# Two heads' attention output as one half-by-half matmul group, with the softmax weights scaled on GpSimd

## The chip, the cores and the metric

The kernel runs on one core of a Trainium2 chip. The metric is the device time of one execution in microseconds (us), as the median of several runs. TensorE (PE in the rows) does matrix products, VectorE (DVE) and ScalarE (ACT) elementwise work and the copies out of PSUM, the accumulator memory; GpSimd (POOL) does a little elementwise work in SBUF, the working memory,. SyncE (SP) issues the weight transfers.

## What is computed

Two layers of a decoder trunk over 512 tokens of width 1024. In each layer one projection feeds four token mixers, whose outputs are gated and summed. The change concerns one of them, sparse attention with 4 heads of 64 dimensions over query blocks of 128 tokens. Cut to what matters:

```python
logits = jnp.einsum('bqhd,bqkhd->bhqk', qb, ks) * (ATT_HD ** -0.5)   # the 128 selected keys of each query
logits = jnp.where(valid[:, None], logits, -jnp.inf)
p = jax.nn.softmax(logits, axis=-1)
y_b = jnp.einsum('bhqk,bqkhd->bqhd', p, vs)                           # -> (512 tokens, 4 heads * 64)
...
merged = merged + gates[:, :, 1] * (y_b @ w_branch[1])
```

The kernel does not gather: it adds a large number to the logits of keys that are not selected, so that block b of queries works on all W = (b+1)*128 keys up to its own.

## The kernel before

All large products go through `mm3`: three passes of a split operand pair (`whi`/`wlo` weights, `hh`/`hl` activations) with 512 columns streaming, in groups called `g` (gate projections), `p` (branch projections), `up`, `dn`, `wo`, `fm`, `tk`. Each engine runs its instructions in the order in which the program stands; the wait for an operand holds up all that is queued behind it on that engine.

The mixers run as generators in the list `side`. `fm_group` calls `tick()` after 4 and after 8 of its 8 weight slices, and each tick advances every generator to its next `yield`. So between two ticks TensorE has either 12 matmuls of `g`, or 6 of `p` and then 12 of `g`. Attention is started ahead of `gates(3, ...)` and one step of it is done at each tick. Its result `yb` is first read by `gates(1, ...)`, a whole gate branch later.

Before, `attention` goes through 16 pairs (block b, head h), four heads in each block. A step i issues, in this order: for every fourth pair `out`, then `values` of pair i-2, `transp` of pair i-1, `softmax` of pair i.

- `softmax`: two matmuls give the logits `lg` in PSUM; DVE adds the selection and takes a row minimum (`L`, `mn`); ACT takes the exponential of `L` and its row sum (`se`); DVE inverts `se`. `L` stays unscaled.
- `transp`: TensorE transposes `L` in blocks of 128 (tile `pT` in PSUM), one ACT copy brings the whole of it to SBUF.
- `values`: for each key block a matmul with the transposed weights in the array and 64 columns of values (`vt`) streaming; result `av` (queries on partitions, 64 columns). DVE scales it by `se` on the way out (`yt`).
- `out`: two transposes (`yT`) turn a block's 256 columns of `yt` back to features on partitions; ACT and DVE split them into `yh` and `yl`.

`mix`, `U` and `br` are small products of other mixers. `mix` and `U` put 64 columns of weights in one half of the array's columns and the next product's in the other half, by the partitions they write (`half(j)`).

Of the kernel before, what the change touches and what calls it, by code (L numbers as in the profile page):

```python
# [13 lines left out]
F32 = mybir.dt.float32  # L14
F32R = mybir.dt.float32r
BF16 = mybir.dt.bfloat16
AF = mybir.ActivationFunctionType
ALU = mybir.AluOpType
# [3 lines left out]
P = 128  # L22
D = 1024
T = 512
# [341 lines left out]
def mixer(tc, em, env):  # L366
# [9 lines left out]
    def et(name):  # L376
        return yp.tile([P, T], F32, name=name, tag="e", bufs=8)

    def ytile(n):
        return (yp.tile([P, 2, T], F32R, name=f"yh{n}", tag="yh", bufs=3),  # L380
                yp.tile([P, 2, T], F32R, name=f"yl{n}", tag="yl", bufs=3))

    tscope = ExitStack()
    tp = tscope.enter_context(tc.tile_pool(name="tp", bufs=1))
    ts = tscope.enter_context(tc.tile_pool(name="ts", bufs=1))

    def tt(shape, name, bufs=1, tag=None):

        p_ = ts if int(np.prod(shape[1:])) % T else tp
        return p_.tile(shape, F32, name=name, tag=tag or name, bufs=bufs)  # L390
# [2 lines left out]
        rs, rb = env["rs"], env["rb"]  # L393

    def rtile(name):
        return tp.tile([P, T], F32R, name=name, tag="ix", bufs=8)

    def half(h):
        return slice((h % 2) * 64, (h % 2) * 64 + 64)

    def blk(c):
        return slice(c * P, (c + 1) * P)
# [18 lines left out]
    def fm_proj():  # L421
        w_h, w_l = next_w()
        pt = mmtile("fm")
        fm_group(pt, w_h, w_l, hh, hl)
        return pt
# [41 lines left out]
    if l > 0:  # L467
        pq = tok_proj(512, G1K, [1, 2, 3], MM4)
    else:

        x0, acc = [], []
        raw01 = yp.tile([P, 2, T], F32R, name="raw01", tag="yh", bufs=3).bitcast(F32)

        def first_loads(k0):
            ks = {0: (0, 1), 1: ()}.get(k0, (k0, k0 + 1))
            for k in ks:
                x0.append(rtile("x0").bitcast(F32))
                with HP():
                    nc.sync.dma_start(x0[k], x_in[k])
                acc[:] = [norm(x0, lp("ln_mix"), hh, hl, (k,), *acc, sq_hp=False, sq_tile=et)]  # L480
            return raw01[:, k0] if k0 < 2 else None

        pq = tok_proj(512, G1K, [1, 2, 3], MM4, first_loads)
        load_consts()
        rs, rb = rstd(acc[0])
# [16 lines left out]
    def table(n):  # L502
# [8 lines left out]
                           ALU.mult, ALU.mult)  # L511
    qiT = {}
    kiT = rtile("kiH"), rtile("kiL")

    def indexer_prep():
# [19 lines left out]
        for c in (1, 2, 3):  # L535
            pk = mmtile("qiT", "ms")
            for j in range(4):
                ptr(pk[:, blk(j)], qr[c][:, blk(j)])

            a, b = qiT[c] = rtile("qiA"), rtile("qiB")  # L540
            lo = et("qiL").bitcast(F32R)
            stack(a, b, pk, (lo[lower], lo[upper]))
            stack_move(a, b, lo[lower], lo[upper])
            yield
# [8 lines left out]
    def indexer(b, sco):  # L553

        W = (b + 1) * P
        for h in range(8):
            pt = mmtile("ix", "ms")
            for i in range(2):
                pmm(pt[:, :W], qiT[b][h % 2][:, blk(h // 2)], kiT[i][:, :W], i == 0, i == 1)
            rel = tt([P, T], "rel", 3, "X")  # L560
            S.activation(rel[:, :W], pt[:, :W], AF.Relu)
            w = wx[:, b, h:h + 1]
            if h == 0:
                V.tensor_scalar(sco[:, :b * P], rel[:, :b * P], w, 0.0, ALU.mult, ALU.add)
                V.scalar_tensor_tensor(sco[:, b * P:], rel[:, b * P:W], w, negP, ALU.mult, ALU.add)
            else:
                V.scalar_tensor_tensor(sco, rel[:, :W], w, sco, ALU.mult, ALU.add)
            if h % 2 == 1:
# [9 lines left out]
        V.tensor_scalar(sco, sco, SENT, BIG, ALU.not_equal, ALU.mult)  # L578

    def attention(sel, yb):  # L580
        yt, Ls, pTs = {}, {}, {}

        def softmax(b, h):
            W = (b + 1) * P
            pt = mmtile("lg", "ms")
            j = h // 2
            q, k = qS[h % 2][:, j, blk(b)], kS[h % 2]
            pmm(pt[:, :W], q, k[:, j, :W], True, False)
            pmm(pt[:, :W], q, kL[h % 2][j][:, :W], False, True)
            L = rtile("L").bitcast(F32)  # L590
            mn = tt([P, 1], "mn", 2)
            se = tt([P, 1], "se", 4)
            V.tensor_tensor_reduce(L[:, :W], pt[:, :W], sel[b], 1.0, 3.4e38, ALU.add, ALU.min, mn)
            S.activation(L[:, :W], L[:, :W], AF.Exp, bias=mn, scale=-1.0, accum_out=se)
            V.reciprocal(se, se)
            Ls[b, h] = (L, se)

        def transp(b, h):
            W = (b + 1) * P
            pk = mmtile("pT", "ms")  # L600
            for s in range(b + 1):
                ptr(pk[:, blk(s)], Ls[b, h][0][:, blk(s)])
            pT = rtile("pT").bitcast(F32)
            S.copy(pT[:, :W], pk[:, :W])
            pTs[b, h] = pT

        def values(b, h):
            if h == 0:
                yt[b] = tt([P, 4, 64], "yt", 2)
            po = mmtile("av", "ms")  # L610
            for s in range(b + 1):
                pmm(po[:, 0:64], pTs[b, h][:, blk(s)], vt[:, s, h * 64:(h + 1) * 64], s == 0, s == b)
            V.tensor_scalar(yt[b][:, h], po[:, 0:64], Ls[b, h][1], None, ALU.mult)

        def out(b):
            pk = mmtile("yT", "ms")
            y2 = yt[b].rearrange("p h d -> p (h d)")
            for j in range(2):
                ptr(pk[:, blk(j)], y2[:, blk(j)])
            pv = pk[:, 0:256].rearrange("p (j t) -> p j t", j=2)  # L620
            yh, yl = yb[0][:, :, blk(b)], yb[1][:, :, blk(b)]
            S.copy(yh, pv)
            V.tensor_sub(yl, pv, yh.bitcast(F32))

        seq = [(b, h) for b in range(4) for h in range(4)]
        for i in range(len(seq) + 3):
            if i >= 3 and seq[i - 3][1] == 3:
                out(seq[i - 3][0])
            if 2 <= i < len(seq) + 2:
                values(*seq[i - 2])  # L630
            if 1 <= i < len(seq) + 1:
                transp(*seq[i - 1])
            if i < len(seq):
                softmax(*seq[i])
            yield
# [160 lines left out]
    def tops():  # L796
        for b, per in ((1, 2), (2, 1), (3, 1)):
# [5 lines left out]
    qS, kS = ([tp.tile([P, 2, T], F32R, name=f"{n}S{r}") for r in range(2)] for n in "qk")  # L803
    hp = env["hpool"]
    kL = ([tp.tile([P, T], F32R, name=f"kL0{j}") for j in range(2)],
          [hp.tile([P, T], F32R, name=f"kL1{j}", tag=("acc", "sq")[j]) for j in range(2)])
# [59 lines left out]
    vt = tt([P, 4, 256], "vt")  # L866
# [10 lines left out]
    for i in range(2):  # L877
        pt = fm_proj()
        with HP():
            V.tensor_mul(cqT[:, i], pt, rb)  # L880
    for i in range(2):
        pt = fm_proj()
# [31 lines left out]
    for c2 in range(2):  # L914
        t = et("gv")
# [34 lines left out]
    for i in range(2):  # L950
        pt = fm_proj()
        u2, t = et("u2"), et("gu")
# [8 lines left out]
    for i in range(2):  # L961
        dc, z, db, t = et("dc"), et("z"), et("db"), et("cv")
        for j, dst in enumerate((dc, z, db)):
            pt = fm_proj()
# [38 lines left out]
    gates(0, ya, 0)  # L1003
    yb = ytile(1)
    side.append(attention(sel, yb))
    gates(3, yd, 1)
    gates(2, yc, 2)
# [9 lines left out]
    for m in range(KD):  # L1017
        w_h, w_l = next_w()
        pt = mmtile("wo")
# [96 lines left out]
```

## Time and profile before

| | |
|---|---|
| median of 3 runs | 1659.71 us (1659.55 to 1659.79) |
| the profiled execution | 1658.94 us |
| its span, first to last instruction | 1657.2 us |
| TensorE busy | 1650.9 us |
| VectorE busy | 956.3 us |
| ScalarE busy | 585.0 us |
| GpSimd busy | 66.0 us |
| mean granted TensorE clock | 0.999 |

The span is what the instructions take; the 1.7 us around it are launch and end. An engine's busy time is the union of its instructions. Of TensorE's instructions the ends are modelled and neighbours overlap, so the steps from one start to the next tell what one costs, not the durations.

### The profile page before, as it was taken

How to read it: one execution, taken by the hardware profiler on the slowest of the kernel's cores; microseconds unless marked ns; L12 is line 12 of the kernel's file. 1: busy time of each engine (PE TensorE's matmuls, PEld its weight loads, DVE VectorE, ACT ScalarE, POOL GpSimd, SP SyncE). 2: the span in 40 equal slices, each digit the busy share in tenths (PEclk: the TensorE clock that was granted, in tenths of full speed). 3: DMA queues.
4: the chain of work that ended last, by engine and by line, in shares of the span. 5: the costliest groups of instructions: out<-in, count | busy, mean ns of one | idle time of the engine just before them, and what ended most of it. 6: DMA issues, size and time to landing. Idle time of an engine off the chain costs nothing.

```text
span 1657.2 us, 20279 instructions
## 1 busy us (share of the span) xinstructions
PE 1650.9 (100%) x7958; PEld 1373.5 (83%) x7958; DVE 956.3 (58%) x1727; ACT 585.0 (35%) x876; POOL 66.0 (4%) x81
## 2 busy tenths in 40 slices
PE   9999999999999999999999999999999999999999
PEld 7888788888888888888888877888888888888888
DVE  6899886555554423443358999855555544334422
ACT  5543233423334312342235432244233343123311
POOL 1311000000000000000012110000000000000000
PEclk9999999999999999999999999999999999999999
DMA  5432222243232323323334222221422323233231
GB/s 205 121 90 90 80 80 80 80 133 98 84 108 89 102 90 101 101 90 121 114 117 121 78 93 92 77 83 64 147 92 89 96 95 102 91 100 101 91 127 64
DMA packets 49296, 164.74 MB, mean 99 GB/s; under 512 B 5680, under 2 KB 8496, under 8 KB 49200
## 3 DMA queue, kind: packets, MB, share of 16 engines
q1 hardware_dynamic: 45072, 158.76, 29.6%
q0 software_dynamic: 3264, 3.67, 1.1%
q8 instruction: 63, 1.03, 0.3%
q10 hardware_dynamic: 864, 1.01, 0.2%
q14 instruction: 33, 0.27, 0.1%
HBM read 155.55 MB, written 4.19 MB: 96 GB/s over the span
## 4 chain that ended last, share of the span: by engine, by line
PE 100%; POOL 0%; ACT 0%; DVE 0%; ACTq 0%; issue 0%
PE g L132 21%; PE dn L132 21%; PE up L132 21%; PE tk L132 10%; PE fm L132 8%; PE p L132 5%; PE wo L132 5%; PE ix L132 1%; PE av L132 1%; PE lg L132 1%; PE pT L132 1%; PE Gb L132 1%; PE intra L132 0%; PE inter L132 0%; PE S L132 0%; PE cols L132 0%
## 5 line engine op out<-in xcount | busy, mean ns | idle before, releaser
L132 ACT CAST whi<-raw 128x1024 fp32r<-128x1024 f32 (+3 forms) x270 | 293.3, 1086 | 636.0 <-PE dn L132 252.0
L132 DVE TENSOR_TENSOR wlo<-raw,whi 128x1024 fp32r<-128x1024 f32 (+3 forms) x270 | 342.2, 1268 | 174.3 <-ACT whi L132 166.6
L132 PE MATMUL dn<-al,whi 128*128 128x512 f32 (+1 forms) x528 | 202.0, 383 | 0.0
L132 PE MATMUL dn<-ah,wlo 128*128 128x512 f32 (+1 forms) x528 | 202.0, 383 | 0.0
L132 PE MATMUL dn<-ah,whi 128*128 128x512 f32 (+1 forms) x528 | 202.0, 383 | 0.0
L132 PE MATMUL g<-hl,whi 128*128 128x512 f32 x512 | 200.6, 392 | 0.0
L132 PE MATMUL g<-hh,whi 128*128 128x512 f32 x512 | 200.6, 392 | 0.0
L132 PE MATMUL g<-hh,wlo 128*128 128x512 f32 x512 | 200.1, 391 | 0.0
L132 PE MATMUL up<-hh,whi 128*128 128x512 f32 x512 | 199.6, 390 | 0.0
L132 PE MATMUL up<-hh,wlo 128*128 128x512 f32 x512 | 199.2, 389 | 0.0
L132 PE MATMUL up<-hl,whi 128*128 128x512 f32 x512 | 199.2, 389 | 0.0
L132 DVE SCALAR_TENSOR_TENSOR u<-up,rb 128x512 f32<-128x512 f32 x64 | 44.1, 691 | 158.9 <-PE up L132 158.9
L132 PEld LDWEIGHTS dn<-al,whi 128*128 128x128 f32 x528 | 99.2, 188 | 19.4
L132 PEld LDWEIGHTS dn<-ah,whi 128*128 128x128 f32 x528 | 99.2, 188 | 19.4
L132 PEld LDWEIGHTS dn<-ah,wlo 128*128 128x128 f32 x528 | 99.2, 188 | 19.2
L132 PEld LDWEIGHTS g<-hh,wlo 128*128 128x128 f32 x512 | 96.3, 188 | 20.3
L132 PEld LDWEIGHTS up<-hh,wlo 128*128 128x128 f32 x512 | 96.1, 188 | 20.1
L132 PEld LDWEIGHTS up<-hl,whi 128*128 128x128 f32 x512 | 96.1, 188 | 20.0
L132 PEld LDWEIGHTS up<-hh,whi 128*128 128x128 f32 x512 | 96.1, 188 | 19.7
L132 PEld LDWEIGHTS g<-hl,whi 128*128 128x128 f32 x512 | 96.2, 188 | 19.6
L132 PEld LDWEIGHTS g<-hh,whi 128*128 128x128 f32 x512 | 96.1, 188 | 19.6
L132 PE MATMUL tk<-whi,hh 128*128 128x512 f32 (+2 forms) x304 | 107.8, 357 | 0.0
(253 smaller groups left out, 2492.2 us busy)
## 6 DMA issues: line engine op xcount, KB each, us to landing
raw<-in_wall_dram SPq DMA_DIRECT2D x194, 512.0 KB, 3.4
raw<-in_wall_dram SPq DMA_DIRECT2D x64, 640.0 KB, 3.9
x<-in_x_dram SPq DMA_DIRECT2D x16, 256.0 KB, 5.0
raw<-in_wall_dram SPq DMA_DIRECT2D x8, 336.0 KB, 2.9
x_dram<-x SPq DMA_DIRECT2D x8, 256.0 KB, 2.0
x<-x_dram SPq DMA_DIRECT2D x8, 256.0 KB, 6.7
out_dram<-x SPq DMA_DIRECT2D x7, 256.0 KB, 2.0
raw<-in_wall_dram SPq DMA_DIRECT2D x4, 256.0 KB, 3.3
```

Of the source, the lines that this page charges most:

```text
L132: r = f(*a, **k)
```

## The change

`attention` now goes by pairs of heads: j is the pair, r the head in it, and the order is j, then block b, then r. A `softmax` ends with a GpSimd instruction that multiplies `L` by the inverted row sum in SBUF; the transposes read that. The transposed weights of all four query blocks of a head are collected in three SBUF tiles (`p0` for key block 0, `p1` for key block 1, `p23` for key blocks 2 and 3), so that `transp` has up to three ACT copies instead of one. `values` is issued twice in a layer, once for each pair of heads: values (64 columns) sit in the array, and 512, 384, 256 or 128 columns of transposed weights stream, head r writing partitions half r. The result has features on partitions already, so `yt`, `out` and its transposes are gone, and one ACT copy and one DVE subtraction of 512 columns make `yh` and `yl`. The buffers of `L` and the transposed weights go from 8 to 9.

```diff
-        return tp.tile([P, T], F32R, name=name, tag="ix", bufs=8)
+        return tp.tile([P, T], F32R, name=name, tag="ix", bufs=9)
...
             V.reciprocal(se, se)
-            Ls[b, h] = (L, se)
-
-        def transp(b, h):
-            W = (b + 1) * P
+            G.tensor_scalar(L[:, :W], L[:, :W], se, None, ALU.mult)
+            Ls[j, b, r] = L
+
+        def transp(j, b, r):
+
             pk = mmtile("pT", "ms")
             for s in range(b + 1):
-                ptr(pk[:, blk(s)], Ls[b, h][0][:, blk(s)])
-            pT = rtile("pT").bitcast(F32)
-            S.copy(pT[:, :W], pk[:, :W])
-            pTs[b, h] = pT
-
-        def values(b, h):
-            if h == 0:
-                yt[b] = tt([P, 4, 64], "yt", 2)
+                ptr(pk[:, blk(s)], Ls[j, b, r][:, blk(s)])
+            if b == 0:
+                pTs[r] = [rtile("pT").bitcast(F32) for _ in range(3)]
+            p0, p1, p23 = pTs[r]
+            S.copy(p0[:, blk(b)], pk[:, blk(0)])
+            if b > 0:
+                S.copy(p1[:, blk(b)], pk[:, blk(1)])
...
+        def values(j):
+
             po = mmtile("av", "ms")
-            for s in range(b + 1):
-                pmm(po[:, 0:64], pTs[b, h][:, blk(s)], vt[:, s, h * 64:(h + 1) * 64], s == 0, s == b)
-            V.tensor_scalar(yt[b][:, h], po[:, 0:64], Ls[b, h][1], None, ALU.mult)
-
-        def out(b):
-            pk = mmtile("yT", "ms")
...
+            for s in range(4):
+                for r in range(2):
+                    p_ = pTs[r][min(s, 2)]
...
+                    h = 2 * j + r
+                    pmm(po[half(r), s * P:], vt[:, s, h * 64:(h + 1) * 64], p_, s == 0, s == 3)
+            yh, yl = yb[0][:, j], yb[1][:, j]
+            S.copy(yh, po)
+            V.tensor_sub(yl, po, yh.bitcast(F32))
...
+        seq = [(j, b, r) for j in range(2) for b in range(4) for r in range(2)]
+        for i in range(len(seq) + 2):
+            if i >= 2 and i % 8 == 1:
+                values(seq[i - 2][0])
```

On TensorE, before, this is a tick in the middle of a gate group with blocks of 512 keys: `g` ends, values of an earlier pair, transposes of the last, logits of the next.

```order
L132 MATMUL g<-hh_95,wlo 128x512
L132 MATMUL av<-vt,pT 128x64 x3
L132 MATMUL pT<-cst,L 128x128 x4
L132 MATMUL lg<-kS_448,qS_446 128x512
L132 MATMUL lg<-kL_451,qS_446 128x512
```

The same place after, at the first pair of heads. The 12 matmuls of `g` ahead of it are all that stands between these transposes and the logits whose softmax they read.

```order
L132 MATMUL g<-hh_95,wlo 128x512
L132 MATMUL pT<-cst,L 128x128 x4
L132 MATMUL lg<-kS_448,qS_446 128x512
L132 MATMUL lg<-kL_451,qS_446 128x512
L132 MATMUL p<-yh_1576,whi 128x512
```

So `av` no longer stands between `g` and the transposes. It stands on TensorE once for each pair of heads, here at the tick after the last logits of the first pair (each row's x2 are the two heads):

```order
L132 MATMUL g<-hh_95,wlo 128x512
L132 MATMUL av<-pT,vt 64x512 x2
L132 MATMUL av<-pT,vt 64x384 x2
L132 MATMUL av<-pT,vt 64x256 x2
L132 MATMUL av<-pT,vt 64x128 x2
L132 MATMUL pT<-cst,L 128x128
L132 MATMUL lg<-kS_448,qS_446 128x128
L132 MATMUL lg<-kL_452,qS_446 128x128
```

In a layer 40 `av` matmuls of 64 columns and 8 `yT` transposes give way to 16 `av` matmuls of 512 to 128 columns. On GpSimd, whose queue had nothing between the last `dn` of another mixer and the next norm's `rs`, the scalings are new:

```order
 L132 TENSOR_TENSOR dn<-dn,nhalf 128x4 x4
+L132 TENSOR_SCALAR L<-L,se 128x128 x2
+L132 TENSOR_SCALAR L<-L,se 128x256 x2
+L132 TENSOR_SCALAR L<-L,se 128x384 x2
+L132 TENSOR_SCALAR L<-L,se 128x512 x2
+L132 TENSOR_SCALAR L<-L,se 128x128 x2
+L132 TENSOR_SCALAR L<-L,se 128x256 x2
+L132 TENSOR_SCALAR L<-L,se 128x384 x2
+L132 TENSOR_SCALAR L<-L,se 128x512 x2
 L132 TENSOR_TENSOR rs<-t_61,nhalf 128x4
```

They are 16 in a layer, one for each softmax, and nothing else is queued among them.

## Rows read from the trace of the kernel before

**Rows 1.** The page: busy time by engine, share of the span, instructions.

```profile
PE 1650.9 (100%) x7958; PEld 1373.5 (83%) x7958; DVE 956.3 (58%) x1727; ACT 585.0 (35%) x876; POOL 66.0 (4%) x81
```

**Rows 2.** Busy time in windows: attention in layer 1 (length, then each engine, clock).

```profile
1079.80:1160.40 80.60, 80.60 (x433) 68.97 (x433) 46.20 (x104) 33.73 (x69) 0.00 (x0) 1.00 0.23 74
```

**Rows 3.** Pieces of the chain that ended last, layer 1's attention: start, us, what.

```profile
1084.92 2.72 PE g L132 x12
1087.65 0.17 PE av L132 x2
...
1107.36 0.39 PE av L132 x4
...
1125.45 0.61 PE av L132 x6
...
1140.66 0.22 PE yT L132 x2
...
1145.39 0.84 PE av L132 x8
```

**Rows 4.** Timeline of TensorE around two small products: start, us, what, how many.

```profile
142.36 0.38 PE L132 MATMUL br<-cst,c_lf 128*4 128x128 f32 x2
142.67 0.27 PE L132 MATMUL br<-cst,c_ip 128*4 128x128 f32 x1
...
148.01 0.39 PE L132 MATMUL fm<-hh,wlo 128*128 128x512 f32 x1
148.33 1.09 PE L132 MATMUL mix<-wt,v 128*64 128x128 f32 x16
...
149.93 0.39 PE L132 MATMUL fm<-hh,wlo 128*128 128x512 f32 x1
```

**Rows 5.** Timeline, a softmax of 512 keys with 12 `g` behind it.

```profile
1133.94 0.16 DVE L132 RECIPROCAL se<-se 128x1 f32<-128x1 f32 x1 [0.94 <-ACT L L132]
...
1134.85 0.78 PE L132 MATMUL av<-vt,pT 128*128 128x64 f32 x6
1135.05 0.69 DVE L132 TENSOR_TENSOR gs<-g,rb 128x512 f32<-128x512 f32 x1 [0.94 <-PE g L132]
```

**Rows 6.** Timeline, the same place with 384 keys.

```profile
1124.16 0.16 DVE L132 RECIPROCAL se<-se 128x1 f32<-128x1 f32 x1 [0.84 <-ACT L L132]
...
1125.29 0.78 PE L132 MATMUL av<-vt,pT 128*128 128x64 f32 x6
```

**Rows 7.** Timeline, 512 keys with 6 `p` and 12 `g` behind.

```profile
1138.63 0.16 DVE L132 RECIPROCAL se<-se 128x1 f32<-128x1 f32 x1
...
1140.49 0.38 PE L132 MATMUL yT<-cst,yt 128*128 128x128 f32 x2
```

**Rows 8.** Timeline, GpSimd waiting for VectorE.

```profile
1054.35 0.16 DVE L132 TENSOR_SCALAR dn<-dn 128x4 f32<-128x4 f32 x1
...
1054.59 1.01 POOL L132 TENSOR_TENSOR dn<-dn,nhalf 128x4 f32<-128x4 f32 x1 [31.82 <-DVE dn L132]
```

**Rows 9.** Timeline, TensorE waiting for GpSimd.

```profile
28.98 1.14 POOL L132 TENSOR_TENSOR rs<-t,nhalf 128x4 f32<-128x4 f32 x1
...
30.17 0.41 PEld L132 LDWEIGHTS pb<-cst,rs 128*128 128x128 f32 x3
30.22 0.44 PE L132 MATMUL pb<-cst,rs 128*128 128x128 f32 x2
```

**Rows 10.** Groups of instructions by form: busy us, mean ns, idle before.

```profile
L132 POOL MEMSET kL<- 64x512 f32 x8 | 4.1, 520 | 349.7 <-PE dn L132 339.9 <-PE pa L132 9.7
...
L132 POOL TENSOR_TENSOR wt<-wt,cst 128x512 f32<-128x512 f32 x2 | 3.7, 1868 | 41.4 <-DMA wt<-in_sgus_dram 41.4
...
L132 POOL TENSOR_SCALAR bb<-bb 128x256 f32<-128x256 f32 x2 | 1.7, 864 | 0.0
```

**Rows 11.** Timeline of GpSimd: a product of two operands while VectorE does nothing.

```profile
80.90 0.63 POOL L132 TENSOR_TENSOR tab<-cst,lp 128x256 f32<-128x256 f32 x1
```

**Rows 12.** Busy time in a window of layer 0 (columns as in rows 2).

```profile
193.20:196.50 3.30, 3.30 (x15) 2.33 (x14) 2.81 (x8) 0.94 (x2) 0.00 (x0) 0.50 0.00 0
```

More of the change, by code (lines that the diff above doesn't have):

```diff
@@ L580, in attention, with softmax @@
     def attention(sel, yb):
-        yt, Ls, pTs = {}, {}, {}
-        def softmax(b, h):
+        Ls, pTs = {}, {}
+        def softmax(j, b, r):
             W = (b + 1) * P
             pt = mmtile("lg", "ms")
-            j = h // 2
-            q, k = qS[h % 2][:, j, blk(b)], kS[h % 2]
+            q, k = qS[r][:, j, blk(b)], kS[r]
             pmm(pt[:, :W], q, k[:, j, :W], True, False)
-            pmm(pt[:, :W], q, kL[h % 2][j][:, :W], False, True)
+            pmm(pt[:, :W], q, kL[r][j][:, :W], False, True)
             L = rtile("L").bitcast(F32)
@@ L615, in out @@
-        def out(b):
-            pk = mmtile("yT", "ms")
[L617 to L630, printed above, removed]
+                ptr(pk[:, blk(s)], Ls[j, b, r][:, blk(s)])
@@ new lines, in transp @@
+            if b == 0:
[4 more added lines that the diff above has]
+                S.copy(p1[:, blk(b)], pk[:, blk(1)])
+            if b > 1:
+                n = b - 1
+                S.copy(p23.rearrange("p (s t) -> p s t", s=2)[:, 0:n, blk(b - 2)],
+                       pk[:, 2 * P:(2 + n) * P].rearrange("p (s t) -> p s t", s=n))
+        def values(j):
+            po = mmtile("av", "ms")
+            for s in range(4):
+                for r in range(2):
+                    p_ = pTs[r][min(s, 2)]
+                    p_ = (p_[:, s * P:] if s < 2 else p_.rearrange("p (s t) -> p s t", s=2)[:, s - 2, (s - 2) * P:])
+                    h = 2 * j + r
[3 more added lines that the diff above has]
+            V.tensor_sub(yl, po, yh.bitcast(F32))
```

## The prediction

> **What bounds the kernel now.** The page comes first: TensorE is busy for 1650.9 us of the span of 1657.2 us [rows 1]. The other engines have room, so an edit counts by what it takes from TensorE's stream and by any wait it puts there. The second view is the busy time in windows. In the attention stage of layer 1, TensorE is busy for all 80.60 us, ScalarE for 33.73 and GpSimd not at all [rows 2]; layer 0 issues the same instructions. The third is the chain that ended last, cut into pieces: since it runs along TensorE, its pieces add up to the time, and a piece can be subtracted. The fourth is the timeline, for the distance from a softmax to the transposes that read it.
>
> **What is removed from TensorE.** A layer has four heads at each of the four block sizes. Their `av` pieces are 0.17, 0.39, 0.61 and 0.84 us [rows 3]; four of each make 4 x 2.01 = 8.04 us. The four pairs of `yT` transposes are 0.22 us each [rows 3], 0.88 us. That is 8.92 us in a layer and 17.84 us in all. VectorE's 32 small scalings and the split by blocks go too, on an engine with room.
>
> **What is added to TensorE.** The old trace has no 512-column product of these unsplit 32-bit operands, but `mix` has the same form: 64 columns of weights in one half of the array, the next product in the other half, here with 128 columns streaming. A `br` matmul stands in the trace as two passes; alone one lasts 0.27 us, and two 0.38 us [rows 4], so a pass follows the other at a step of 0.11 us. A `mix` block has 16 passes. One after the other they would last 0.27 + 15 x 0.11 = 1.92 us, in pairs 0.27 + 7 x 0.11 = 1.04; the row says 1.09 [rows 4]. So the two halves run side by side. With columns, the step grows in proportion: 0.44, 0.33, 0.22 and 0.11 us for the four key blocks, 1.10 us for a pass over all of them, 2.20 us for both passes, and both heads fit into that. Going into the half-array form and back also costs: from 148.01 to 149.93 lie one `mix` block and three `fm` steps [rows 4] of 2.72/12 = 0.227 us [rows 3], so the block takes 1.92 - 0.68 = 1.24 us, of which eight steps are 0.88; 0.36 is left. One `values` is 2.20 + 0.36 = 2.56 us, and four are 10.24 us. The bounds: if a 512-column pass went at the 0.227 us of a `g` matmul, four would cost 4 x (1.14 + 0.36) = 6.0 us; if the heads went one after the other, 4 x (4.40 + 0.36) = 19.0 us. I take the value by `mix`, the one row with the same operand type and half-array form. TensorE's work shrinks by 17.84 - 10.24 = 7.6 us.
>
> **What the scaling on GpSimd adds.** It is new on the way from softmax to transposes. Before, a transposition waited for the exponential alone, with the inverted sum beside it; now it waits for the inversion, the hand-over to GpSimd, the product and the hand-over to TensorE. Softmaxes of head r = 0 have 12 `g` behind them, those of r = 1 have 6 `p` more.
>
> With 512 keys and r = 0, the inversion ends at 1134.10, and TensorE is ready for the next attention work at 1134.85 [rows 5]; after the change the first of that is the transposes. VectorE hands over to GpSimd in 0.08 us (1054.51 to 1054.59) [rows 8], and GpSimd to TensorE in 0.10 us, weight load included (30.12 to 30.22) [rows 9]. That leaves GpSimd 0.57 us. With 384 keys (1124.32 to 1125.29) [rows 6] it has 0.79 us, and with 512 keys and r = 1 (1138.79 to 1140.49) [rows 7] 1.52 us. Smaller blocks have more room than the same place at 384.
>
> No row shows GpSimd multiply 512 columns by a scalar per partition. From below: setting 512 columns takes 0.52 us, reading nothing [rows 10]. From above: a product of two operands of 512 columns took 1.87 us [rows 10]. VectorE is idle from 1134.10 to 1135.05 [rows 5], and with VectorE idle a two-operand product of 256 columns took 0.63 us [rows 11], 1.26 us for 512 if all of it scaled. One operand is read here, so I take the middle of 0.52 and 1.26, 0.89 us; for 384 columns 0.67 us. TensorE then waits 0.89 - 0.57 = 0.32 us at each 512-key softmax of r = 0, and not with 384. There are four (two pairs of heads, two layers): 1.3 us. Behind the waiting transposes stand the next logits and `g`, so the wait is lost whole. By the ends it is nothing, or, at 1.26 us (0.95 for 384 keys), 4 x (0.69 + 0.16) = 3.4 us.
>
> The Trainium skill, "GPSIMD Engine Reference", section "Performance versus the Vector engine", speaks against such a move: elementwise work runs about half as fast there as on VectorE, and it gives 769 ns for a tight loop over 512 elements. No run here shows that loop; by its figure the wait would be 4 x 0.20 = 0.8 us and the time 0.5 us under mine.
>
> **What costs nothing.** ScalarE's extra copies (three of 128 or 256 columns in place of one of 512) stand on an engine that is busy for 33.73 of 80.60 us [rows 2], and are first read by `values` a tick later, over 2.72 us behind [rows 3]; without that cover each would delay `values` by a few tenths. Six of the nine buffers hold collected weights and three rotate among the `L`, each released by transposes two ticks before it is needed again. `yb` is read a gate branch later.
>
> **Sum.** 7.6 - 1.3 = 6.3 us off. The profiled execution took 1658.94 us, so 1652.6; the median of the runs is 0.77 above that execution, so **1653.4 us**.
>
> **The rivals.**
> - *GpSimd takes the gain back, no change.* At 1.87 us for 512 columns [rows 10] and 1.40 for 384, TensorE waits 1.30 and 0.61 us with r = 0 and 0.35 with r = 1, 4 x 2.26 = 9.0 us, so 1661.1 us. For it: a one-operand product of 256 columns, `bb`, took 0.86 us [rows 10], and twice that is 1.73. Against: VectorE is idle here. Chance 0.10.
> - *The same wait, longer: slower.* The three waits add to 2.75p - 2.88 us for p us per 512 columns, four times. At p = 1.74 the 7.6 us are gone; over 2.04 the kernel is slower by more than 0.2%. At 2.3 it is 13.8 us of waiting, 1665.9 us. For it: GpSimd's cost with a scalar per partition has no row. Against: no product among the rows is so slow. Chance 0.06.
> - *The heads do not overlap.* 19.0 us in place of 10.24: 8.8 us more, 1662.2 us. Against: `mix`. For: its streams are short. Chance 0.05.
> - *The clock falls once more.* In layer 0 TensorE was granted half its clock (0.50, 1.2 in place of 2.4 GHz) for some 3.3 us [rows 12]. A stretch of half-array products, or layer 1 arriving earlier, may bring another: 3.3 us at half speed loses 1.7 us, so 1655.1 us. Chance 0.15.
>
> **The numbers.** My forecast has 0.60, from 1652.1 (no waiting) to 1655.5 (3.4 us of it); other causes have 0.04. The range takes in the clock on top and the nearer part of the first rival: 1651.5 to 1658 us. A measurement of this kernel can tell about 0.2%, 3.3 us, so faster means under 1656.4. The forecast and the clock, with some of the rest, give 0.77 for faster; most of the first and third rival 0.16 for the same; 0.07 for slower.
>
> **What would show it.** Right: 16 `av` passes in pairs in each `values`, the first pairs some 0.44 us apart, a whole block near 2.5 us; no `yT`; and on TensorE a short wait with `L` from GpSimd as its releaser at 512 keys alone. Wrong: a GpSimd product of 512 columns well off 0.9 us, such a wait at smaller blocks, steps of 0.22 or 0.88 us between the wide passes, or a second stretch at granted clock 0.50.

## The result

The changed kernel takes 1670.41 us (median of 4 runs, 1670.1 to 1671.67) and the kernel before, on the same chip, 1659.75 (1659.55 to 1660.48): a ratio of 1.0067, interval 1.0055 to 1.008. It is 10.7 us slower; the forecast was 1653.4, so 17.0 us are to be found.

The page of the changed kernel (its profiled execution took 1670.46 us, a span of 1668.4): the busy time by engine, and the shares of the chain that ended last.

```profile
PE 1646.1 (99%) x7846; PEld 1356.2 (81%) x7846; DVE 949.6 (57%) x1691; ACT 586.6 (35%) x912; POOL 115.1 (7%) x113
...
PE 78%; POOL 2%; DVE 1%; ACT 1%; issue 1%; POOLq 0%; DVEq 0%; ACTq 0%
```

Against [rows 1], TensorE is busy for 4.8 us less while the span is 11.2 us longer: it now stands still. GpSimd, with 32 instructions and 49 us more, has entered the chain with 2%. The view of waits names the place: for whom TensorE waited, us in all, times, longest.

```profile
PE pT L132 <- POOL L L132: 15.2, 20, 1.3
```

The `values` block, timeline of TensorE (a row with a count runs from its first matmul's start to its last one's end):

```profile
1125.58 0.39 PE L132 MATMUL g<-hh,wlo 128*128 128x512 f32 x1
1125.90 2.38 PE L132 MATMUL av<-pT,vt 128*64 128x512 f32 x16
1128.20 0.33 PE L132 MATMUL pT<-cst,L 128*128 128x128 f32 x1
```

From the last `g` to the first instruction behind the block are 2.62 us, which is one ordinary step of 0.227 and 2.39 for the block, where 2.56 was forecast. So the new product is as cheap as was thought. The loss is at the new wait. At 512 keys and head r = 0, in the place of [rows 5]:

```profile
1114.87 0.16 DVE L132 RECIPROCAL se<-se 128x1 f32<-128x1 f32 x1 [0.88 <-ACT L L132]
...
1115.20 1.57 POOL L132 TENSOR_SCALAR L<-L,se 128x512 f32<-128x512 f32 x1 [3.13 <-DVE se L132]
...
1115.51 0.39 PE L132 MATMUL g<-hh,wlo 128*128 128x512 f32 x1
...
1116.82 0.42 PEld L132 LDWEIGHTS pT<-cst,L 128*128 128x128 f32 x4 [1.34 <-POOL L L132]
```

TensorE starts the transposes 1.31 us behind its last `g` instead of 0.23: 1.08 us are lost. The hand-overs are near the forecast (0.17 us to GpSimd and 0.05 to the weight load, for 0.08 and 0.10); the product takes 1.57 us, not 0.89. And a wait stands where none was forecast, at 384 keys of r = 1:

```profile
1108.84 0.15 DVE L132 RECIPROCAL se<-se 128x1 f32<-128x1 f32 x1
...
1108.95 0.69 DVE L132 TENSOR_TENSOR mg<-mg,gs 128x512 f32<-128x512 f32 x1
...
1109.16 2.92 POOL L132 TENSOR_SCALAR L<-L,se 128x384 f32<-128x384 f32 x1 [3.36 <-DVE se L132]
...
1109.56 1.48 DVE L132 TENSOR_TENSOR wlo<-raw,whi 128x1280 fp32r<-128x1280 f32 x1
...
1112.13 0.31 PEld L132 LDWEIGHTS pT<-cst,L 128*128 128x128 f32 x3 [1.71 <-POOL L L132]
```

384 columns, fewer than above, last 2.92 us, and they end about a microsecond behind `wlo`, though nothing of this product depends on `wlo`. At r = 0, where VectorE at that time runs `gs<-g,rb` (its operand `g` in PSUM), the same 384 columns take 1.25 us. In the kernel before, VectorE's timeline has the same two instructions behind the inversion of [rows 7], at 512 keys of r = 1:

```profile
1138.75 0.69 DVE L132 TENSOR_TENSOR mg<-mg,gs 128x512 f32<-128x512 f32 x1
1139.37 1.49 DVE L132 TENSOR_TENSOR wlo<-raw,whi 128x1280 fp32r<-128x1280 f32 x1
```

The groups by form, in the changed kernel, put both heads together:

```profile
L132 POOL TENSOR_SCALAR L<-L,se 128x384 f32<-128x384 f32 x8 | 16.7, 2082 | 23.9 <-DVE se L132 21.3 <-issue 2.6
L132 POOL TENSOR_SCALAR L<-L,se 128x256 f32<-128x256 f32 x8 | 14.1, 1764 | 27.8 <-DVE se L132 27.8
L132 POOL TENSOR_SCALAR L<-L,se 128x512 f32<-128x512 f32 x8 | 13.9, 1744 | 26.8 <-DVE se L132 26.8
L132 POOL TENSOR_SCALAR L<-L,se 128x128 f32<-128x128 f32 x8 | 4.9, 609 | 40.9 <-DVE se L132 31.0 <-PE p L132 9.9
```

A mean of 2.08 us for 384 columns and 1.74 for 512 can't be a rate. Undisturbed the products take 0.61, 0.93, 1.25 and 1.57 us: 0.30 us and 2.5 ns a column. At r = 1 those of 256, 384 and 512 columns take 2.60, 2.92 and 1.92.

One measure serves for all kernels below: **attention work on TensorE in a layer**, the time from the last `g` or `p` before each block of attention matmuls to the first one behind it, less 0.227 us, added up over the blocks of a layer from the timeline. It is 18.14 us before and 23.84 after, 5.70 more in each of two layers: 11.4 us, all of the loss (11.2 by the spans; the stretch at half the clock of [rows 12] is absent from this execution, and its first attention block begins 0.4 us earlier). By the start of the waiting transposes, a pair of heads loses at r = 0 0.50 us (384 keys) and 1.08 (512), and at r = 1 1.12 (256), 1.45 (384) and 0.45 (512); over four pairs that is 6.3 and 12.1 us.

### The profile page after: what moved, and what is told of

The parts are those of the page before. It is cut to its first block, busy times and chain, and to the rows that moved or that the text cites. A ratio compares the mean times of both kernels' runs of the same rounds, so it can differ in the third digit from the quotient of the medians.

```text
span 1668.4 us, 20080 instructions
## 1 busy us (share of the span) xinstructions
PE 1646.1 (99%) x7846; PEld 1356.2 (81%) x7846; DVE 949.6 (57%) x1691; ACT 586.6 (35%) x912; POOL 115.1 (7%) x113
## 4 chain that ended last, share of the span: by engine, by line
PE 78%; POOL 2%; DVE 1%; ACT 1%; issue 1%; POOLq 0%; DVEq 0%; ACTq 0%
PE dn L132 21%; PE up L132 21%; PE g L132 14%; PE wo L132 5%; PE tk L132 5%; PE fm L132 4%; PE p L132 4%; POOL L L132 2%; PE pT L132 1%; PE av L132 1%; DVE gs L132 1%; PE ix L132 1%; ACT L L132 0%; PE lg L132 0%; DVE L L132 0%
```

## The experiments

The theory: the product form gives its 7.6 us, and TensorE's wait for GpSimd costs more than that, partly by GpSimd's own rate, partly because VectorE's instructions with two operands in SBUF keep GpSimd from reading. The rivals: the product, the copies or the clock cost something too; or GpSimd's work loads the chip wherever it stands; or it is simply slow beside any work of VectorE's.

**Without the scaling.**

```
             V.reciprocal(se, se)
-            G.tensor_scalar(L[:, :W], L[:, :W], se, None, ALU.mult)
             Ls[j, b, r] = L
```

> The changed kernel without the scaling, so that the attention output is not divided by its row sums. Theory A: nothing waits, 1659.75 - 7.6 = 1652 us, the price of the new form alone; the transposes wait for ScalarE's exponential, which ends before TensorE comes to them. Theory B: above 1657 us.

Measured: 1652.14 us (1651.81 to 1652.6, 4 runs), ratio 0.9954 (0.9941 to 0.9968). Attention work is 14.12 us a layer, 4.02 under before: 8.0 us, and 7.4 by the medians (1659.49 for the kernel before in the same batch). The prediction subtracted 7.6. So without the scaling the change takes off what was forecast; the whole loss came with the scaling.

**The scaling on VectorE.**

```
-            G.tensor_scalar(L[:, :W], L[:, :W], se, None, ALU.mult)
+            V.tensor_scalar(L[:, :W], L[:, :W], se, None, ALU.mult)
```

> The changed kernel with one word altered: the scaling of L stands on VectorE in place of GpSimd. Theory A (the loss is TensorE waiting for GpSimd's product, whose time and hand-over exceed the gap to the transposes): VectorE needs at most the 0.69 us of its 512-column sums and no hand-over behind the inversion, so the waits go and the work taken off TensorE, 7.6 us, shows: about 1652 to 1653.5 us. Theory B (the new form of the values, the three copies on ScalarE or the order by pairs of heads delays TensorE too): a good part of the 10.7 us stays, above 1657 us.

Measured: 1655.8 us (1654.26 to 1657.27, 10 runs), ratio 0.9976 (0.9966 to 0.9985): faster than before, but by half of what the product form gives; theory A's 1652 to 1653.5 us was missed, since waits are left. Attention work is 16.01 us. VectorE scales 512 columns in 0.49 us, but takes its instructions in order. Timeline of VectorE at 384 keys, r = 1:

```profile
1102.14 0.15 DVE L132 RECIPROCAL se<-se 128x1 f32<-128x1 f32 x1
1102.26 0.69 DVE L132 TENSOR_TENSOR mg<-mg,gs 128x512 f32<-128x512 f32 x1
1102.87 1.48 DVE L132 TENSOR_TENSOR wlo<-raw,whi 128x1280 fp32r<-128x1280 f32 x1
1104.27 0.41 DVE L132 TENSOR_SCALAR L<-L,se 128x384 f32<-128x384 f32 x1
```

The scaling stands behind `mg` and `wlo` in the queue and starts 2.0 us behind the inversion's end: on either engine the same two instructions are in its way. (This edit also let the scheduler put three `g` ahead of some transposes, so it is not a clean price of that place.)

**The scaling on GpSimd in the kernel before** (the old form else; the copy out of `av` multiplies by one).

```
             V.reciprocal(se, se)
+            G.tensor_scalar(L[:, :W], L[:, :W], se, None, ALU.mult)
             Ls[b, h] = (L, se)
...
-            V.tensor_scalar(yt[b][:, h], po[:, 0:64], Ls[b, h][1], None, ALU.mult)
+            V.tensor_scalar(yt[b][:, h], po[:, 0:64], 1.0, None, ALU.mult)
```

> The kernel before with the GpSimd scaling alone added behind the inversion (the later scaling multiplies by 1). Theory A: TensorE waits again, but less, since before each group of transposes stand 0.17 to 0.84 us of av, and sometimes 0.22 of yT: with the GpSimd times of the changed kernel some 1.7 us in a layer are left, so 1661 to 1666 us. Theory B: the scaling is not the cause, and the time stays at 1659.7.

Measured: 1663.04 us (1660.62 to 1663.64, 10 runs), ratio 1.0018 (1.0009 to 1.0027). The same 32 products cost here only 1.03 us a layer of attention work (19.17). They are the undisturbed ones for 384 columns and under:

```profile
L132 POOL TENSOR_SCALAR L<-L,se 128x384 f32<-128x384 f32 x8 | 10.0, 1244 | 28.8 <-DVE se L132 28.8
...
L132 POOL TENSOR_SCALAR L<-L,se 128x256 f32<-128x256 f32 x8 | 7.4, 925 | 26.7 <-DVE se L132 26.7
```

At 384 columns of every second head (r = 1 in the changed kernel) VectorE's order is another one here: `gs<-gs,p`, with its operand `p` in PSUM, stands between the inversion and `mg`.

```profile
1122.28 0.67 DVE L132 SCALAR_TENSOR_TENSOR gs<-gs,p 128x512 f32<-128x512 f32 x1
...
1122.53 1.25 POOL L132 TENSOR_SCALAR L<-L,se 128x384 f32<-128x384 f32 x1 [2.78 <-DVE se L132]
...
1122.98 0.69 DVE L132 TENSOR_TENSOR mg<-mg,gs 128x512 f32<-128x512 f32 x1
```

`gs<-gs,p` was under way when GpSimd began and held up nothing; `mg` came 0.45 us after GpSimd, and neither of the two took longer than alone. So GpSimd's work costs little by itself; what costs is when it falls.

The attention work explains 2.1 of the 3.6 us by the medians (1659.49 for the kernel before in the same batch). In the profiled execution the granted clock was 0.66 between 1020 and 1025 us, where the kernel before had 1.00: behind the recurrent mixer's small products `S` and `ktok` the `p` matmuls follow each other at 0.43 us in place of 0.227. That is 1.7 us outside the attention stage; the three executions of 1660.6 to 1660.9 us have the higher mean clock, 1.000 in place of 0.998 or 0.999.

**The same work, read a tick later.** Transposes and `values` each wait for one softmax more.

```
-        for i in range(len(seq) + 2):
-            if i >= 2 and i % 8 == 1:
-                values(seq[i - 2][0])
-            if 1 <= i < len(seq) + 1:
-                transp(*seq[i - 1])
+        for i in range(len(seq) + 3):
+            if i >= 3 and i % 8 == 2:
+                values(seq[i - 3][0])
+            if 2 <= i < len(seq) + 2:
+                transp(*seq[i - 2])
```

> The changed kernel with the transposes (and the values behind them) one tick later, so that two gaps lie between a softmax and its transposes; GpSimd does the same work. Theory A, a wait for one result: the longest GpSimd product, 2.9 us, fits into the two gaps, and the time is 1652 to 1653.5 us. Rival C (GpSimd's work as such costs time, by slowing VectorE's instructions through a shared way to SBUF, and these hold TensorE): no less than 1657 us.

Measured: 1652.04 us (1651.74 to 1652.45, 4 runs), ratio 0.9954 (0.994 to 0.9967). Attention work is 14.03 us and the view of waits has no row of TensorE on `L`, though the products are as long as in the changed kernel:

```profile
L132 POOL TENSOR_SCALAR L<-L,se 128x384 f32<-128x384 f32 x8 | 16.6, 2080 | 16.6 <-DVE se L132 16.6
...
L132 POOL TENSOR_SCALAR L<-L,se 128x512 f32<-128x512 f32 x8 | 13.9, 1742 | 15.8 <-DVE se L132 15.8
```

It is as fast as with no scaling at all (1652.14), so the loss is the wait and nothing else. This version beats both kernels: 0.5% under the one before.

**Later, and on VectorE**: the edits of the two kernels above together.

> The kernel with the later transposes, the scaling on VectorE in place of GpSimd. Theory A (only the wait counts, and two gaps hide either engine): within 0.2% of 1652.04 us, as with GpSimd. If GpSimd's products still cost something when nobody waits for them, up to 2 us less.

Measured: 1652.26 us (1651.79 to 1652.6, 4 runs), ratio 0.9956 (0.9939 to 0.9972); attention work 14.03. With a tick of room the engine does not matter.

**`wlo` in two instructions** (for the gate's chunks of 1280 columns), in the changed kernel.

```
-                V.tensor_sub(lo[:, :L], raw[:, :L], hi[:, :L].bitcast(F32))
+                for c0 in ((0, L // 2) if L == WCH else (0,)):
+                    c1 = c0 + (L // 2 if L == WCH else L)
+                    V.tensor_sub(lo[:, c0:c1], raw[:, c0:c1], hi[:, c0:c1].bitcast(F32))
```

> The changed kernel with VectorE's subtraction wlo of the gate chunks done as two instructions of 640 columns in place of one of 1280. In the changed kernel a GpSimd product of 384 columns takes 1.25 us when wlo is not there and 2.92 when it is; of 256 columns 0.93 and 2.60. Theory A1 (a VectorE instruction with two operands in SBUF shuts GpSimd's product out until it ends): GpSimd comes in between the halves, the long products shorten by about 0.7 us, eight waits of TensorE with them, and the time falls by some 5 us to 1665. Theory A2 (both only share a bandwidth): the product stays at 2.6 and 2.9 us and the time at 1670.4 or a little above, for 64 more instructions.

Measured: 1670.33 us (1668.8 to 1670.93, 4 runs), ratio 1.0064 (1.0049 to 1.0079): no gain in time. But the products did get shorter, at r = 1 to 1.93 us for 256 columns and 2.25 for 384 (0.67 less each, a half of `wlo`), and the means with them:

```profile
L132 POOL TENSOR_SCALAR L<-L,se 128x384 f32<-128x384 f32 x8 | 14.0, 1747 | 23.9 <-DVE se L132 21.3 <-issue 2.6
...
L132 POOL TENSOR_SCALAR L<-L,se 128x256 f32<-128x256 f32 x8 | 11.4, 1429 | 27.9 <-DVE se L132 27.9
```

Attention work fell to 21.19 us, 5.3 less over both layers. It was given back elsewhere. Busy time in windows (the granted clock is the column behind POOL):

```profile
194.00:199.00 5.00, 5.00 (x22) 3.76 (x21) 3.67 (x12) 1.97 (x3) 1.01 (x1) 0.66 0.00 0
229.00:233.00 4.00, 4.00 (x12) 3.20 (x11) 2.50 (x6) 0.63 (x2) 0.00 (x0) 0.57 0.02 4
1058.00:1062.50 4.50, 4.50 (x19) 3.52 (x19) 2.79 (x8) 0.42 (x1) 0.00 (x0) 0.62 0.05 22
```

In each of these the clock stood at its lower level (1.2 in place of 2.4 GHz) for part of the window; in the first, the `p` matmuls right behind the small products `S` and `ktok` follow each other at 0.43 us in place of 0.227. The three cost 5.00 x 0.34 + 4.00 x 0.43 + 4.50 x 0.38 = 5.1 us, where the changed kernel's execution was granted 1.00; waits of `br` and `hT` on VectorE in the recurrent stage add 1.2. Such stretches differ from one execution to the next of a kernel; why this one had more is open. A verdict on time alone would have thrown away a right mechanism.

**The heads' products one head after the other**, in the version with the tick, to test the rival that they might not overlap.

```
-            for s in range(4):
-                for r in range(2):
+            for r in range(2):
+                for s in range(4):
```

> The kernel with the later transposes (1652.04 us), its eight av matmuls of a pair of heads issued head by head in place of in turn. If the two halves of the array run side by side only because neighbours in the stream address different halves, a block takes 2.2 us more, four of them 8.8, so about 1661 us. If TensorE reaches past four matmuls to the other half, 1652 us.

Measured: 1658.36 us (1656.95 to 1658.95, 10 runs), ratio 0.9992 (0.9983 to 1.0002), 6.3 us over the version with the tick. The block, on TensorE's timeline:

```profile
1119.77 3.93 PE L132 MATMUL av<-pT,vt 128*64 128x512 f32 x16
```

It lasts 3.93 us in place of 2.38, four times: 6.2 us, between the two forecasts and nearer the first. So the forecast's pairs are real, and to have them in full they must be written in pairs. It is not quite the sum of two heads (4.40): the first 512-column pass of the second head starts while three shorter passes of the first are still to come.

**Only r = 0 on VectorE**, in the changed kernel; TensorE's order is untouched.

```
-            G.tensor_scalar(L[:, :W], L[:, :W], se, None, ALU.mult)
+            if r == 1:
+                G.tensor_scalar(L[:, :W], L[:, :W], se, None, ALU.mult)
+            else:
+                V.tensor_scalar(L[:, :W], L[:, :W], se, None, ALU.mult)
```

> The changed kernel with the softmaxes of head r = 0 scaled on VectorE and those of r = 1 on GpSimd as before; TensorE's order of instructions is that of the changed kernel. Theory A (two separate losses: 6.3 us in which TensorE waits for GpSimd's own rate at r = 0, and 12.0 us at r = 1, where VectorE's two-operand instructions keep GpSimd out): the r = 0 waits go and the r = 1 waits stay, so 1670.4 - 6.3 = 1664.1 us, with GpSimd products of 2.60, 2.92 and 1.92 us for 256, 384 and 512 columns at r = 1. Rival B (one loss: the late r = 0 products push the r = 1 softmaxes into VectorE's weight preparation): with r = 0 on time the r = 1 products fall toward their undisturbed 0.93, 1.25 and 1.57 us and most of the 12.0 us goes too: 1653 to 1657 us.

Measured: 1669.63 us (1669.36 to 1671.73, 5 runs), ratio 1.0062 (1.0049 to 1.0074). Both theories missed: the waits at r = 0 are gone, yet little was won. At 512 keys of r = 1:

```profile
1120.59 0.15 DVE L132 RECIPROCAL se<-se 128x1 f32<-128x1 f32 x1
...
1120.71 0.69 DVE L132 TENSOR_TENSOR mg<-mg,gs 128x512 f32<-128x512 f32 x1
...
1120.91 3.24 POOL L132 TENSOR_SCALAR L<-L,se 128x512 f32<-128x512 f32 x1 [7.14 <-DVE se L132]
...
1121.32 1.48 DVE L132 TENSOR_TENSOR wlo<-raw,whi 128x1280 fp32r<-128x1280 f32 x1
```

This product takes 3.24 us, in the changed kernel 1.92:

```profile
1120.16 0.69 DVE L132 TENSOR_TENSOR mg<-mg,gs 128x512 f32<-128x512 f32 x1
...
1120.37 1.92 POOL L132 TENSOR_SCALAR L<-L,se 128x512 f32<-128x512 f32 x1 [3.60 <-DVE se L132]
...
1120.83 1.92 DVE L132 TENSOR_TENSOR wlo<-raw,whi 128x1280 fp32r<-128x1280 f32 x1
```

In the changed kernel GpSimd got in between `mg` and `wlo` here, and it was `wlo` that grew, from 1.48 to 1.92; in this one `wlo` starts 0.61 us behind `mg`'s start, not 0.67, and GpSimd stays out. The wait grows from 0.45 to 1.76 us, which is 1.31 lost of the 1.58 won at r = 0 in each pair. The two losses are not separate: who comes first between two of VectorE's instructions decides over 1.3 us. (That the 0.06 us are the gap in which GpSimd got in is read from these rows, not tried.)

**`wlo` from one operand**: the low halves of the gate's chunks are made as `whi` times zero (so the gate is computed from the high halves alone), by a form that lasts as long, 1.48 us. The same edit was run twice: first with its extra column `wsum` in the pool of the weights, then in the small buffers.

```
-                V.tensor_sub(lo[:, :L], raw[:, :L], hi[:, :L].bitcast(F32))
+                if L == WCH:
+                    V.tensor_scalar(lo[:, :L], hi[:, :L].bitcast(F32), 0.0, None, ALU.mult,
+                                    ALU.add, accum_out=wsum)
+                else:
+                    V.tensor_sub(lo[:, :L], raw[:, :L], hi[:, :L].bitcast(F32))
...
```

> The changed kernel, but for weight chunks of 1280 columns VectorE makes wlo from one SBUF operand (whi times zero, with the row sum written out beside it) in place of raw minus whi, so the low halves of these weights are zero and the gate is computed from the high halves alone; TensorE's order in the attention stages is unchanged (in the recurrent stage before it a few dozen instructions trade places). mg, with two SBUF operands and 0.69 us, stays. Theory A (it is the second SBUF operand of VectorE's instruction that keeps GpSimd out): at r = 1 a product waits for mg at most and then runs beside wlo, so 0.93, 1.25, 1.57 us plus up to 0.65: about 1.6, 1.9 and 1.6 us for 256, 384 and 512 columns; TensorE's waits at r = 1 fall from 12.0 to about 2.5 us, so about 1661 us. Rival B (any VectorE instruction of that length beside it slows GpSimd): the products stay at 2.6 and 2.9 us, the waits at 12 us, and the time at 1670 us.

Measured: 1688.93 us (1688.33 to 1689.31, 5 runs), ratio 1.0174 (1.0161 to 1.0188). The products and the waits moved as the theory said (means of 1.10, 1.42 and 1.74 us, attention work 18.47 us), and something else cost over 20 us. `g` and `up` had become slower, so the extra column alone was put into the changed kernel:

```
+        wsum = wpool.tile([P, 1], F32, name="wsum", tag="wsum", bufs=1)
         off = [0]
...
-            se = tt([P, 1], "se", 4)
+            se = tt([P, 1], "se", 3)
```

> The changed kernel with an unused column of 4 bytes a partition put ahead of the weight buffers (and three buffers in place of four for the row sums), so that buffers behind it start 32 bytes later; no instruction is added and TensorE's order is unchanged. In the kernel whose gate weights' low halves were made from one operand, the g and up matmuls took 395 to 399 ns each in place of 389 to 391. If the moved addresses did that (theory A), they do so here: 3072 matmuls by about 6.5 ns are 20 us, so about 1690 us. If it came from the zero low halves or the 64 extra read-outs on VectorE (rival B), this kernel stays at 1670 us.

Measured: 1694.38 us (1693.59 to 1698.04, 5 runs), ratio 1.0211 (1.0197 to 1.0225), 24 us over the changed kernel with the same number of instructions on every engine. TensorE's groups by form:

```profile
L132 PE MATMUL g<-hh,whi 128*128 128x512 f32 x512 | 203.3, 397 | 0.0
...
L132 PE MATMUL up<-hh,whi 128*128 128x512 f32 x512 | 202.8, 396 | 0.0
...
L132 PE MATMUL dn<-ah,whi 128*128 128x512 f32 x496 | 193.0, 389 | 0.0
```

In the changed kernel these are 391, 390 and 389 ns. The moved addresses did it (three buffers for the row sums are in the next kernel too, where `g` and `up` take 389 to 393 ns), and the edit could be tried without them:

> The kernel whose gate weights' low halves are made from one operand (low halves zero, the gate computed from the high halves alone), with its extra column in the small buffers behind, so that no other buffer moves. Theory A (two-operand instructions of VectorE keep GpSimd out; the 20 us lost elsewhere in that kernel came from moved addresses): products of 1.10, 1.42 and 1.74 us in the mean for 256, 384 and 512 columns, 5.4 us a layer less for the attention work on TensorE than in the changed kernel, so 1670.4 - 10.7 = 1659.7 us, plus or minus 3 us for the instructions that trade places in the recurrent stage. Rival B (the 20 us came with the one-operand instruction itself): the products are the same, and the time is 1689 us.

Measured: 1665.98 us (1665.25 to 1667.37, 5 runs), ratio 1.0036 (1.0024 to 1.0049). `wlo` is still there, as long as ever, beside the same products:

```profile
L132 POOL TENSOR_SCALAR L<-L,se 128x512 f32<-128x512 f32 x8 | 13.9, 1742 | 26.9 <-DVE se L132 26.9
L132 POOL TENSOR_SCALAR L<-L,se 128x384 f32<-128x384 f32 x8 | 11.4, 1422 | 24.5 <-DVE se L132 21.7 <-issue 2.8
L132 POOL TENSOR_SCALAR L<-L,se 128x256 f32<-128x256 f32 x8 | 8.8, 1103 | 27.8 <-DVE se L132 27.8
```

At r = 1, 384 columns now take 1.60 us in place of 2.92:

```profile
1108.08 0.69 DVE L132 TENSOR_TENSOR mg<-mg,gs 128x512 f32<-128x512 f32 x1
...
1108.28 1.60 POOL L132 TENSOR_SCALAR L<-L,se 128x384 f32<-128x384 f32 x1 [3.38 <-DVE se L132]
...
1108.68 1.48 DVE L132 TENSOR_SCALAR_CACHE_REDUCE wlo<-whi 128x1280 fp32r<-128x1280 f32 x1
```

The 0.35 us over the undisturbed 1.25 are put down to `mg` in front: at 256 and 512 columns it is the same 0.35. Attention work is 18.83 and 18.90 us in the two layers, 9.95 less in all. The time fell by 4.4 only, and theory A's 1659.7 us was missed, for reasons in the recurrent stage, where the scheduler let instructions trade places: TensorE's waits there,

```profile
PE inter L132 <- DVE X L132: 3.0, 4, 1.1
...
PE br L132 <- DVE X L132: 0.7, 2, 0.4
PE U L132 <- DVE yl L132: 0.4, 2, 0.2
```

are 4.1 us that the changed kernel does not have. From 210 to 215 us the granted clock was besides 0.66, with `g` at steps of 0.43 us behind the mixer's products `inter`, where the changed kernel had 1.00: another 1.7 us.

So it is not the length of `wlo` that keeps GpSimd out. The edit takes away its second SBUF operand and, with it, the operation (a product with a read-out in place of a difference). That the operand decides is argued from `gs<-gs,p` above, which has two operands but one of them in PSUM, and was under way beside a product of 1.25 us; no run changes the operand alone.

The Trainium skill, "SBUF — State Buffer", section "Who interferes with whom", states this rule: a VectorE instruction with two SBUF inputs contends with a GpSimd instruction that reads SBUF. The rows of 2.92 us (two operands) and 1.60 us (one) agree. The section also calls the shared pair of ports an exclusive lock, and says of VectorE's two-port modes that whoever issues first has the pair for the whole instruction and the other fully blocks. For GpSimd behind `wlo` a full block fits: 2.92 us end 1.0 us behind `wlo`, about the 0.95 that 384 columns take without the constant 0.30. In the other order it does not: `wlo` beside a product of 1.92 us grew by 0.44 us, not by the 1.46 for which GpSimd still ran, and `mg` inside the product of 1.25 us did not grow at all; here the measurement decides.

## Why the prediction was wrong, by its steps

- **What is removed, what is added: right.** 7.6 us were forecast; without the scaling the kernel is 7.4 us faster by the medians and 8.0 by its attention work. A block of `values` took 2.39 us for 2.56. The step of a wide product taken from `mix` [rows 4] held, and so did the overlap of the two heads.
- **What the scaling on GpSimd adds: the step that failed.** In two places.
  - The price. "I take the middle of 0.52 and 1.26, 0.89 us" is 1.57. None of [rows 10] and [rows 11] was a product with a scalar per partition, and the nearest in operation, `bb` with 0.86 for 256 columns, was used for a rival only: it is within 0.07 of the 0.93 measured. The budgets were right: with 1.57 and 1.25 us they give waits of 1.57 - 0.57 = 1.00 and 1.25 - 0.79 = 0.46, and 1.08 and 0.50 were measured. This cost 6.3 us for the forecast's 1.3; alone it would have made 1652.1 + 6.3 = 1658.4, no change. The Trainium skill's 769 ns ("GPSIMD Engine Reference", "Performance versus the Vector engine") was half of what this form took; again the measurement decides.
  - The company. "Smaller blocks have more room than the same place at 384" goes by places of r = 0, where VectorE is idle or reads PSUM. At r = 1 one place was read, for its length alone [rows 7], though `mg` and `wlo` stand right behind its inversion. In the changed kernel they follow the inversion at once at 256 and 384 keys as well, and the product waits for them: 12.1 us, where the forecast had nothing. Without the second operand of `wlo` 10.0 us of attention work go, so this is what took the kernel from no change to slower.
- **What costs nothing: right.** The copies, the buffers and the later `yb` left no wait: the kernel without the scaling has the forecast gain to within 0.4 us.
- **The rivals.** The first, 1661.1 us by a longer product, had the right place for a third of the loss. The one that ended slower had a right sign by a rate of 2.04 us or more for 512 columns; the rate stayed below that, and the loss came at the smaller blocks, which it left out. The heads do overlap, and the clock did not fall once more: in the changed kernel's profiled execution the granted clock was 1.00 even in the place of [rows 12].
- **What would show it: wrong** as listed there: a product well off 0.9 us and a wait at smaller blocks.

## What to carry to other kernels

Before work goes to GpSimd, read for each place where it will run what VectorE does at that moment, and how many of that instruction's operands lie in SBUF; one place read does not speak for the other head of the same loop. Where a wait is new on a path, the cheapest remedy may be to read its result one step later: here this was worth 18 us, more than any choice of engine. And a small kernel edit can move buffers or the clock; compare the stage as well as the time.

## What was not expected of the hardware

- GpSimd multiplied by a scalar per partition at 0.30 us and 2.5 ns a column, VectorE the same 512 columns in 0.49 us: 1.57 against that is a factor of 3.
- 4 bytes a partition ahead of the weight buffers made `g` and `up`, 3072 matmuls, 6 ns longer each, about 19 of the 24 us; `fm`, `tk` and `p` of 512 columns, 2 to 5 ns longer each, have most of the rest, while `dn` and `wo`, with weights from the same buffers, stayed at 389. The granted clock of that execution was 0.999. Which of the moved buffers does this, and why, is open.
- With a VectorE instruction of two SBUF operands (`mg`, 0.69 us) under way first, GpSimd's products were 0.35 us longer; where GpSimd had begun 0.45 us before `mg`, neither was.
- Matmuls in the two halves of the array, issued head by head, overlapped in part (3.93 us, between 2.38 and 4.40).
